# Differential attention in a two-layer decoder trunk: the order of mixing and rotation on VectorE, coefficients of three score tiles in one instruction, and rotary weight columns laid out by parity

## The chip, the cores and the metric

The kernel runs on one core of one Trainium2 chip. The metric is the device time of one execution in microseconds (us). A core has a matrix engine (TensorE, PE in the profile, with its weight loads as PEld), a vector engine (VectorE, DVE), an activation engine (ScalarE, ACT), a general engine (GpSimd, POOL) and a queue for transfers (SyncE, SP). Each works through its own list of instructions in the order in which it was written; engines wait for each other through semaphores.

## What is computed

The trunk has two layers over 512 tokens of width 1024. Each layer is a half-step SwiGLU feed-forward block, a token mixer, a cross-attention into 256 memory tokens and a second feed-forward block, each followed by a layer norm. The mixer of layer 0 is the differential attention; that of layer 1 is a pooling mixer. The change lies in the attention alone:

```python
q, k, v = jnp.split(x @ w_qkv, 3, axis=-1)          # 8 heads, two halves of 64 for q and k
q, k = rope(q, cos, sin), rope(k, cos, sin)          # pairs (c, c + 32) in each half of 64
s = einsum('bqhcd,bkhcd->bhcqk', q, k) * 64 ** -0.5  # causal, two score maps per head
p = softmax(s, axis=-1)
a = p[:, :, 0] - lam * p[:, :, 1]                    # the mix
o = einsum('bhqk,bkhe->bqhe', a, v)                  # then a norm per head, and @ w_o
```

All is float32. Products are made of two float32r parts: a high part (a rounded copy) and a low part (the rest), and three matmuls of parts take the place of one.

## The kernel before

The attention runs as two streams that one loop weaves into each other. The main stream (`da_main`) projects, for each pair of heads, the values `v` (two PSUM tiles of two token tiles each) and then per head the query `q` and the key `k`, each over 8 slices of the width in 24 matmuls. For the last pair of heads the values come after the keys. The side stream (`da_side`) does the attention of a head that was projected some time before: scores (`sc`) and their masks with the row maximum, exponentials, mix, transposes of the mixed tiles (`pt` from `p`), product with the values (`po`), scaling (`o`), and the turn of the head before (`pt` from `o`, then `oT`). A clock of estimated matmul time says after how many matmuls of the main stream the next step of the side stream is put in.

A head has four score tiles (query tiles 0 to 3), which are 128, 256, 384 and 512 columns wide, with two maps `p[0]` and `p[1]` each. For each map VectorE subtracts the mask and finds the maximum (`L1171`), and ScalarE takes the exponential and its row sum (`L1174`) into `sd`. `da_mix` then makes, per tile, a reciprocal `rc` of one sum (`L1187`), a coefficient `cf` (`L1188`), and `p[0] = p[1] * cf + p[0]` (`L1189`). It is told to stand behind the last mask of the head, and nothing else. TensorE then transposes the mixed tile (`L506`, `pt` from `p`), ScalarE and VectorE split the result into high and low part (`a`, `L135` and `L136`), and TensorE multiplies these by the values (`L1210`, `L1211`).

Rotation (`da_rope`) of a projected query or key: VectorE swaps the partners within groups of 32 partitions (`L1129`, a stream shuffle from PSUM), multiplies the projection by the cosines (`L1130`, the last reader of the PSUM tile), GpSimd multiplies the swapped copy by the signed sines (`L1131`), and VectorE adds the two (`L1132`, the rotary sum). ScalarE and VectorE then split the sum into parts (`L140` and `L141` for a query, `L135` and `L136` for a key).

For partners to lie 16 partitions apart, `cols_rope` reorders the columns of the weights while it splits them: ScalarE makes the high part of 128x1024 (`L290`), VectorE the low part in two halves of 128x512 (`L293`). Heads 0 to 5 use these lines; the same function serves heads 6 and 7.

The projections `q`, `k`, `v` and later the sums `ps` share one pool of two PSUM tiles. A third projection takes the tile whose readers are taken to be done first, and its first matmul waits for them.

What sets the order: a scheduler writes each engine's list before the program runs, from the order of the code, from dependencies and from costs that it assumes. `issue_after(x)` and `queue_behind(y, x)` say that an instruction may not stand ahead of `x` on its engine, with no wait. `high_priority()` puts instructions ahead of others that are free at the same point.

Of the kernel before, what the change touches and what calls it, by code (L numbers as in the profile page):

```python
# [9 lines left out]
F32 = mybir.dt.float32  # L10
# [3 lines left out]
ALU = mybir.AluOpType  # L14
# [3 lines left out]
P = 128  # L18
D = 1024
S = 512  # L20
NT = S // P
# [64 lines left out]
def shape_constants():  # L86

    p = np.arange(P)
    ident = np.eye(P, dtype=np.float32)
    mask = np.where(p[None, :] > p[:, None], np.float32(NEG), np.float32(0.0)).astype(np.float32)  # L90

    quarter, half, e = (p // 32) % 2, (p // 16) % 2, p % 16
    inv = np.array(INV_FREQ_BITS, dtype=np.uint32).view(np.float32)
    rope = np.stack([inv[quarter * 16 + e], np.where(half == 0, -1.0, 1.0)], axis=1).astype(np.float32)

    band = np.zeros((P, 4, 2, BAND), np.float32)
    t = np.arange(BAND)
# [12 lines left out]
def drain(units):  # L110
    for _ in units:
        pass
# [7 lines left out]
class Trunk:  # L120
# [80 lines left out]
    def mm(self, name):  # L201
        return self.mmp.tile([P, S], F32, tag="mm", name=name)
# [81 lines left out]
    def cols_rope(self, raw, j, wait=False):  # L284

        nc = self.nc
        w = self.hl([P, 8, P])
        src = raw[:, j].rearrange("p k (m h q e) -> p (k m) q h e", m=2, h=2, q=2)
        hi, lo = (t.rearrange("p k (m q h e) -> p (k m) q h e", m=2, q=2, h=2) for t in w)
        nc.scalar.copy(hi, src)  # L290
        with self.tc.issue_after(self.turned[1].ins) if wait else nullcontext():
            for q in range(2):
                self.last_low = nc.vector.tensor_sub(  # L293
                    lo[:, :, q], src[:, :, q], hi[:, :, q].bitcast(F32)
                )
        return w

    def wide(self, raw):
# [827 lines left out]
    def da_rope(self, ps):  # L1126
        nc = self.nc
        t1, t2 = self.tmp("rt"), self.tmp("rt")
        nc.vector.stream_shuffle(t2, ps, [(i + 16) % 32 for i in range(32)])  # L1129
        nc.vector.tensor_tensor(t1, ps, self.ropeC, ALU.mult)  # L1130
        nc.gpsimd.tensor_tensor(t2, t2, self.ropeS, ALU.mult)  # L1131
        nc.vector.tensor_tensor(t1, t1, t2, ALU.add)  # L1132
        return t1

    def da_query(self, ps):
# [11 lines left out]
    def da_scores(self, st, before):  # L1147

        nc = self.nc
        q, k, mm, terms = st["q"], st["k"], self.nc.tensor.matmul, ((0, 0), (1, 0), (0, 1))  # L1150
        one, two, three = ([self.aux("sc") for m in range(2)] for i in range(3))
        banks = {
            0: [t[:, 3 * P :] for t in two],
            1: [t[:, : 2 * P] for t in one],
            2: [t[:, : 3 * P] for t in two],
            3: three,
        }
        for i in SC_ORDER:
            qi, kn = slice(i * P, (i + 1) * P), slice(0, (i + 1) * P)
            for a, b in terms:  # L1160
                for m, rows in enumerate(HALVES):
                    mm(banks[i][m], q[a][rows, qi], k[b][rows, kn], start=a == b, stop=b == 1)
        for i in SC_ORDER:
            n = (i + 1) * P
            mx, rc, cf = self.small("mx"), self.small("rc", (P, 1)), self.small("cf", (P, 1))
            sm = st["sm"][:, i]
            p = [self.tmp("p")[:, :n] for m in range(2)]
            with self.tc.high_priority():
                for m in range(2):
                    least = mx[:, m : m + 1]  # L1170
                    st["masked"] = nc.vector.tensor_tensor_reduce(  # L1171
                        p[m], banks[i][m], self.mask[:, S - n :], -1.0, -NEG, ALU.add, ALU.min, least
                    )
                    exp = nc.scalar.activation(  # L1174
                        p[m], p[m], AF.Exp, bias=least, scale=-1.0, accum_out=sm[:, m : m + 1]
                    )
                if i == 2 and before:
                    with self.tc.issue_after(exp.ins):
                        self.da_scale(before)
            st["m", i] = p, sm, rc, cf  # L1180

    def da_mix(self, st, i):

        nc = self.nc
        p, sm, rc, cf = st.pop(("m", i))
        with self.tc.issue_after(st["masked"].ins):
            nc.vector.reciprocal(rc, sm[:, 1:2])  # L1187
            nc.vector.scalar_tensor_tensor(cf, sm[:, 0:1], self.nlam, rc, ALU.mult, ALU.mult)  # L1188
            nc.vector.scalar_tensor_tensor(p[0], p[1], cf, p[0], ALU.mult, ALU.add)  # L1189
        st["p", i] = p[0]  # L1190

    def da_turn(self, st, i):
# [55 lines left out]
    def da_main(self):  # L1248

        w, w_o = self.a["da_w_qkv"][0], self.a["da_w_o"][0]  # L1250
        self.turn_late(1)
        for n in range(0, DA_H, 2):
            vs = []
            if n < V_FIRST:
                yield from self.da_values(n, vs)
            rq, rk = self.raw_heads(w, n * P), self.raw_heads(w, D + n * P)
            for h in range(n, n + 2):
                q = self.mm("q")
                ws = self.cols_rope(rq, h % 2, h == 0)
                yield from self.project(q, ws)  # L1260
                q = self.da_query(q)
                k = self.mm("k")
                ws = self.cols_rope(rk, h % 2, h == 0)
                if h == 0:
                    with self.tc.issue_after(self.last_low.ins):
                        self.nlam = self.lam()
                yield from self.project(k, ws)
                k = self.da_key(k)
                sm = self.small("sd", (P, NT, 2))
                self.heads.append((self.clock, {"h": h, "q": q, "k": k, "v": vs, "sm": sm}))  # L1270
            if not vs:
                yield from self.da_values(n, vs)
        yield from self.to_tokens(self.oT[:4], w_o, 0, 4, True, False, ALPHA)
# [26 lines left out]
    def diff_attention(self, layer, ln):  # L1300
        self.mask = self.act("mask", (P, S), mybir.dt.bfloat16)
        self.nc.gpsimd.memset(self.mask[:, : S - P], 0.0)
        self.nc.gpsimd.tensor_copy(self.mask[:, S - P :], self.maskr)
        self.heads, self.oT = [], [None] * DA_H
        self.weave(self.da_main(), self.da_side(), GAP)
# [459 lines left out]
```

## Time and profile before

| | us |
|---|---|
| median of 3 runs | 1912.29 |
| lowest and highest | 1911.85 and 1914.07 |
| span of the profiled execution | 1913.0 |
| TensorE busy in it | 1894.9 (99%) |
| VectorE busy in it | 1550.6 (81%) |
| ScalarE busy in it | 1003.8 (52%) |
| granted TensorE clock, mean | 0.999 of full |

The attention takes about 345 to 560 us of the span. In the rows of the timeline the first number is the start in us from the span's start, the second the duration; then come engine, line, operation, output and inputs, shape and count, and in brackets how long the engine stood idle before it and what released it. An engine may begin its next instruction a little before the recorded end of the last one: on VectorE some 0.08 us, on ScalarE some 0.1 us, and TensorE's matmuls of 512 columns begin 0.23 us apart and are drawn 0.39 us long.

### The profile page before, as it was taken

Reading aid. Unit: us, or ns where it says so; the run is one execution under the profiler, and the core shown is the slowest. Engines: PE = TensorE matmul, PEld = TensorE weight load, DVE = VectorE, ACT = ScalarE, POOL = GpSimd, SP = SyncE. Lnnn points to the kernel's source line nnn. Section 1 sums busy time; section 2 is a strip of 40 time slices with the busy share of each in tenths; the row PEclk is TensorE's granted clock in tenths of the full one; section 3 lists DMA queues with packets and bytes.
Section 4 is the critical chain, followed back from the end, with each engine's and each line's share of the span. In section 5 each row is a group of like instructions: output and inputs, shape, how many; then the busy total and the mean of one; then the engine's idle time right before and its main releaser. Section 6 shows DMA issues by size and latency. Waiting matters only on the chain.

```text
span 1913.0 us, 32564 instructions
## 1 busy us (share of the span) xinstructions
PE 1894.9 (99%) x13136; PEld 1733.1 (91%) x13136; DVE 1550.6 (81%) x2250; ACT 1003.8 (52%) x1546; POOL 317.3 (17%) x274
## 2 busy tenths in 40 slices
PE   9999999999999999999999999999999999999998
PEld 8999998888878888999998999999899889999997
DVE  7888889888867558889888988898787568898886
ACT  6555554566645435645554655455455436555552
POOL 3112120111110001221220311212130012211210
PEclk9999999999999999999999999999999999999999
DMA  9978772323225327987785687878344438877861
GB/s 248 216 166 187 166 146 82 91 67 89 89 67 155 111 66 198 182 179 162 144 192 179 109 179 165 183 163 184 111 133 133 134 87 171 178 159 166 188 132 56
DMA packets 246743, 277.96 MB, mean 145 GB/s; under 512 B 8256, under 2 KB 212544, under 8 KB 246592
## 3 DMA queue, kind: packets, MB, share of 16 engines
q0 software_dynamic: 92928, 92.29, 31.5%
q1 hardware_dynamic: 153664, 183.59, 30.0%
q8 instruction: 103, 1.69, 0.4%
q14 instruction: 48, 0.39, 0.1%
HBM read 273.75 MB, written 2.10 MB: 144 GB/s over the span
## 4 chain that ended last, share of the span: by engine, by line
PE 85%; DVE 10%; ACT 2%; DMA 1%; issue 1%; POOL 1%; SPq 0%; DVEq 0%; ACTq 0%; POOLq 0%
PE x L221 7%; PE x L220 7%; PE x L222 7%; PE ps L220 4%; PE z L221 4%; PE z L220 4%; PE z L222 4%; PE ps L222 4%; PE ps L221 4%; PE px L222 2%; PE px L220 2%; PE px L221 2%; PE pt L506 2%; PE y L222 2%; PE x L757 2%; PE xq L222 2%
## 5 line engine op out<-in xcount | busy, mean ns | idle before, releaser
L725 POOL DMA_DIRECT2D ra<-in_ffn_w_in_dram x132 | 170.7, 1314 | 982.3 <-DVE wl L732 966.5
L730 ACT CAST wh<-ra 128x1024 fp32r<-128x1024 f32 x176 | 185.1, 1053 | 208.0 <-PE x L221 63.3
L732 DVE TENSOR_TENSOR wl<-ra,wh 128x1024 fp32r<-128x1024 f32 x176 | 214.4, 1223 | 66.5 <-ACT wh L730 66.1
L220 PE MATMUL x<-xe,wh 128*128 128x256 f32 x704 | 195.0, 277 | 0.0
L221 PE MATMUL x<-xe,wh 128*128 128x256 f32 x704 | 194.8, 277 | 0.0
L222 PE MATMUL x<-xe,wl 128*128 128x256 f32 x704 | 194.8, 277 | 0.0
L730 ACT CAST wh<-rc 128x1024 fp32r<-128x1024 f32 x132 | 139.0, 1053 | 102.4 <-PE x L221 41.6
L135 ACT CAST wh<-b 128x1024 fp32r<-128x1024 f32 x112 | 117.8, 1052 | 130.4 <-PE x L221 66.1
L732 DVE TENSOR_TENSOR wl<-rc,wh 128x1024 fp32r<-128x1024 f32 x132 | 160.3, 1222 | 25.5 <-ACT wh L730 25.5
L136 DVE TENSOR_TENSOR wl<-b,wh 128x1024 fp32r<-128x1024 f32 x112 | 136.9, 1222 | 41.0 <-ACT wh L135 41.0
L220 PE MATMUL x<-xh,wh 128*128 128x256 f32 x536 | 148.7, 277 | 0.0
L221 PE MATMUL x<-xl,wh 128*128 128x256 f32 x536 | 148.3, 277 | 0.0
L222 PE MATMUL x<-xh,wl 128*128 128x256 f32 x536 | 148.3, 277 | 0.0
L220 PEld LDWEIGHTS x<-xe,wh 128*128 128x128 f32 x704 | 132.4, 188 | 1.3
L221 PEld LDWEIGHTS x<-xe,wh 128*128 128x128 f32 x704 | 132.3, 188 | 1.3
L222 PEld LDWEIGHTS x<-xe,wl 128*128 128x128 f32 x704 | 132.2, 188 | 0.0
L136 DVE TENSOR_TENSOR wl<-raw,wh 128x1024 fp32r<-128x1024 f32 x64 | 82.4, 1296 | 41.1 <-ACT wh L135 40.5
L221 PEld LDWEIGHTS x<-xl,wh 128*128 128x128 f32 x536 | 100.8, 188 | 0.7
L220 PEld LDWEIGHTS x<-xh,wh 128*128 128x128 f32 x536 | 100.7, 188 | 0.7
L222 PEld LDWEIGHTS x<-xh,wl 128*128 128x128 f32 x536 | 100.6, 188 | 0.0
L135 ACT CAST wh<-raw 128x1024 fp32r<-128x1024 f32 x64 | 66.4, 1049 | 61.0 <-PE xq L221 19.1
L220 PE MATMUL z<-xe,wh 128*128 128x256 f32 x352 | 97.5, 277 | 0.0
(447 smaller groups left out, 6266.0 us busy)
## 6 DMA issues: line engine op xcount, KB each, us to landing
ra<-in_ffn_w_in_dram POOLq DMA_DIRECT2D x132, 512.0 KB, 7.0
rc<-in_ffn_w_in_dram SPq DMA_DIRECT2D x88, 512.0 KB, 5.8
b<-in_ffn_w_out_dram SPq DMA_DIRECT2D x76, 512.0 KB, 4.8
ra<-in_ffn_w_in_dram SPq DMA_DIRECT2D x44, 512.0 KB, 4.7
rc<-in_ffn_w_in_dram POOLq DMA_DIRECT2D x44, 512.0 KB, 7.8
raw<-in_xa_wkv_dram SPq DMA_DIRECT2D x16, 1024.0 KB, 5.4
raw<-in_da_w_qkv_dram SPq DMA_DIRECT2D x16, 512.0 KB, 5.2
raw<-in_xa_wq_dram SPq DMA_DIRECT2D x8, 1024.0 KB, 5.7
```

What stands on the lines that cost most here:

```text
L135: self.nc.scalar.copy(hi, src),
L136: self.nc.vector.tensor_sub(lo, src, hi.bitcast(F32)),
L220: self.first_mm = mm(out, w[0], x[0], start=start, stop=False, skip_group_check=again)
L221: mm(out, w[0], x[1], start=False, stop=False, skip_group_check=again)
L222: self.last_mm = mm(out, w[1], x[0], start=False, stop=stop, skip_group_check=again)
L506: self.turns = [self.nc.tensor.transpose(pt[:, j], b, self.ident) for j, b in enumerate(blocks)]
L725: nc.gpsimd.dma_start(t, source(*block), accum_op=ALU.add)
L730: hi = nc.scalar.copy(v[0], raw)
L732: lo = nc.vector.tensor_sub(v[1], raw, v[0].bitcast(F32))
L757: self.last_mm = nc.tensor.matmul(ps[:, j], v[i][:, k, j * P : (j + 1) * P], x[l][:, k], start=n == i == l == 0, stop=n == 7 and i == 1, s ...
```

## The change

Four things are changed, all in the attention:

- `da_mix` makes the reciprocals and coefficients of tiles 0 to 2 in one instruction of 128x3 each, and those of tile 3 in one of 128x1. All of the mix has high priority.
- The rotary sum of a query that was projected before the scores of the head ahead of it is put behind the mix of tile 2.
- The columns of the rotary weights are reordered by parity (even columns in the first 32 partitions, odd ones in the next 32), so that the low part is one instruction of 128x1024. Its source is read with a step of two elements, as is that of the high part.
- The table of frequencies follows the new order.

```diff
-    rope = np.stack([inv[quarter * 16 + e], np.where(half == 0, -1.0, 1.0)], axis=1).astype(np.float32)
+    rope = np.stack([inv[2 * e + quarter], np.where(half == 0, -1.0, 1.0)], axis=1).astype(np.float32)
...
-        src = raw[:, j].rearrange("p k (m h q e) -> p (k m) q h e", m=2, h=2, q=2)
-        hi, lo = (t.rearrange("p k (m q h e) -> p (k m) q h e", m=2, q=2, h=2) for t in w)
+        src = raw[:, j].rearrange("p k (m r q) -> p (k m) q r", m=2, q=2)
+        hi, lo = (t.rearrange("p k (m q r) -> p (k m) q r", m=2, q=2) for t in w)
         nc.scalar.copy(hi, src)
         with self.tc.issue_after(self.turned[1].ins) if wait else nullcontext():
-            for q in range(2):
-                self.last_low = nc.vector.tensor_sub(
-                    lo[:, :, q], src[:, :, q], hi[:, :, q].bitcast(F32)
-                )
+            self.last_low = nc.vector.tensor_sub(lo, src, hi.bitcast(F32))
         return w
...
-        nc.vector.tensor_tensor(t1, t1, t2, ALU.add)
+        self.rope_sum = nc.vector.tensor_tensor(t1, t1, t2, ALU.add)
...
-            st["m", i] = p, sm, rc, cf
+            st["m", i] = p
+        self.scored += 1
+        st["late_sums"], self.late_sums = self.late_sums, []
...
-        p, sm, rc, cf = st.pop(("m", i))
-        with self.tc.issue_after(st["masked"].ins):
-            nc.vector.reciprocal(rc, sm[:, 1:2])
-            nc.vector.scalar_tensor_tensor(cf, sm[:, 0:1], self.nlam, rc, ALU.mult, ALU.mult)
-            nc.vector.scalar_tensor_tensor(p[0], p[1], cf, p[0], ALU.mult, ALU.add)
+        p = st.pop(("m", i))
+        with self.tc.high_priority(), self.tc.issue_after(st["masked"].ins):
+            if i in (0, NT - 1):
+                n = slice(0, NT - 1) if i == 0 else slice(i, NT)
+                rc, st["cf"] = self.small("rc", (P, NT)), self.small("cf", (P, NT))
+                rc, cf, sm = rc[:, n], st["cf"][:, n], st["sm"][:, n]
+                nc.vector.reciprocal(rc, sm[:, :, 1])
+                nc.vector.scalar_tensor_tensor(cf, sm[:, :, 0], self.nlam, rc, ALU.mult, ALU.mult)
+            cf = st["cf"][:, i : i + 1]
+            mixed = nc.vector.scalar_tensor_tensor(p[0], p[1], cf, p[0], ALU.mult, ALU.add)
+        if i == NT - 2:
+            for add in st["late_sums"]:
+                self.queue_behind(add, mixed)
         st["p", i] = p[0]
...
                 q = self.da_query(q)
+                if self.scored < h:
+                    self.late_sums.append(self.rope_sum)
```

What the scheduler makes of it shows in the engines' lists. The lines of the changed kernel are numbered up to 9 apart from those before: the shuffle is `L1126`, the rotary sum `L1129`, the mix `L1189` to `L1192`.

VectorE around the masks of head 2, before: the rotation of the query of head 3 stands ahead of the first mask, and the first tile to be mixed is tile 0 (128 columns).

```order
L1130 TENSOR_TENSOR rt<-q,ropeC 128x512
L293 TENSOR_TENSOR wl<-raw,wh 128x16x32
L1132 TENSOR_TENSOR rt<-rt 128x512
L293 TENSOR_TENSOR wl<-raw,wh 128x16x32
L141 SCALAR_TENSOR_TENSOR qk<-rt,qk 128x512
L1171 ISA p,mx<-sc,mask 128x128
...
L1187 RECIPROCAL rc<-sd 128x1 x3
L1188 SCALAR_TENSOR_TENSOR cf<-sd,nlam,rc 128x1 x2
L1189 SCALAR_TENSOR_TENSOR p<-p,cf 128x128
L1189 SCALAR_TENSOR_TENSOR p<-p,cf 128x256
L1188 SCALAR_TENSOR_TENSOR cf<-sd,nlam,rc 128x1
L1187 RECIPROCAL rc<-sd 128x1
```

The same place in the change:

```order
L1127 TENSOR_TENSOR rt<-q,ropeC 128x512
L292 TENSOR_TENSOR wl<-raw,wh 128x1024
L1167 ISA p,mx<-sc,mask 128x128
...
L1189 RECIPROCAL rc<-sd 128x3
L1190 SCALAR_TENSOR_TENSOR cf<-sd,nlam,rc 128x3
L1192 SCALAR_TENSOR_TENSOR p<-p,cf 128x256
L1192 SCALAR_TENSOR_TENSOR p<-p,cf 128x384
L1189 RECIPROCAL rc<-sd 128x1
L1192 SCALAR_TENSOR_TENSOR p<-p,cf 128x128
L1190 SCALAR_TENSOR_TENSOR cf<-sd,nlam,rc 128x1
L1129 TENSOR_TENSOR rt<-rt 128x512
L1192 SCALAR_TENSOR_TENSOR p<-p,cf 128x512
```

The sum and the split of the query have moved behind the mix, and tile 0 is mixed last of the first three, behind the reciprocal of tile 3. That order of the tiles is the same in all eight heads; the late sum is there in heads 0, 2, 4, 5 and 6.

TensorE at head 6, where the main stream projects the values of heads 6 and 7 (two tiles, `v_5736` and then `v_5867` in the change). Before, the second projection follows the first at once, and the transposes of head 6 stand between its matmuls; here are its last matmul ahead of the first transpose, and that transpose:

```order
L222 MATMUL v_5939<-wh_5792,xl_3487 128x256
L506 MATMUL pt_5961<-ident_78,p_5875 128x128 [waits DVE_49]
L220 MATMUL v_5939<-wh_5796,xh_3486 128x256
L221 MATMUL v_5939<-wl_5797,xh_3486 128x256
L222 MATMUL v_5939<-wh_5796,xl_3488 128x256
```

In the change all 14 transposes stand in one block between the two projections, and the first matmul of the second waits:

```order
L222 MATMUL v_5736<-wh_5732,xl_3488 128x256
L503 MATMUL pt_5907<-ident_78,p_5816 128x128 [waits DVE_49]
L503 MATMUL pt_5907<-ident_78,p_5816 128x128
L503 MATMUL pt_5978<-ident_78,p_5823 128x128 [waits DVE_49]
...
L503 MATMUL pt_6005<-ident_78,p_5834 128x128 [waits DVE_49]
L503 MATMUL pt_6005<-ident_78,p_5834 128x128 x3
L220 MATMUL v_5867<-wh_5728,xh_3485 128x256 [waits DVE_49,PE_49]
L221 MATMUL v_5867<-wl_5729,xh_3485 128x256
```

The instruction that this matmul waits for is VectorE's part of the split of the first projection: the second now takes the PSUM tile of the first, and no longer that of a key. At head 5 the lists moved in the same way: transposes and value products of head 5 that stood between matmuls of a key's projection now stand in one block ahead of it, and that projection's first matmul waits for VectorE.

VectorE at head 6, before, behind the mix of tile 2, and then in the change, behind the mix of tile 0 (`v` is the split in question):

```order
L1189 SCALAR_TENSOR_TENSOR p<-p,cf 128x384
L1188 SCALAR_TENSOR_TENSOR cf<-sd,nlam,rc 128x1
L1189 SCALAR_TENSOR_TENSOR p<-p,cf 128x512
L136 TENSOR_TENSOR v<-v 128x4x128
L136 TENSOR_TENSOR a<-pt,a 128x128
```

```order
L1129 TENSOR_TENSOR rt<-rt 128x512
L1192 SCALAR_TENSOR_TENSOR p<-p,cf 128x512
L136 TENSOR_TENSOR a<-pt,a 128x128
L1126 STREAM_SHUFFLE rt<-k 128x512
L136 TENSOR_TENSOR a<-pt,a 128x256
L141 SCALAR_TENSOR_TENSOR qk<-rt,qk 128x512
L136 TENSOR_TENSOR v<-v 128x4x128
L1127 TENSOR_TENSOR rt<-k,ropeC 128x512
```

The split of the values has moved behind a rotary sum, two splits of transposes, a shuffle of a key and the split of a query.

More of the change, by code (lines that the diff above doesn't have):

```diff
@@ L1164, in da_scores @@
             n = (i + 1) * P
-            mx, rc, cf = self.small("mx"), self.small("rc", (P, 1)), self.small("cf", (P, 1))
-            sm = st["sm"][:, i]
+            mx, sm = self.small("mx"), st["sm"][:, i]
             p = [self.tmp("p")[:, :n] for m in range(2)]
@@ L1304, in diff_attention @@
         self.heads, self.oT = [], [None] * DA_H
+        self.scored, self.late_sums = 0, []
         self.weave(self.da_main(), self.da_side(), GAP)
```

## The prediction

> **What bounds the kernel now.** The page comes first, then TensorE's waits inside the attention (330 to 600 us), then the timeline of the engines at each of its eight heads.
>
> ```profile
> PE 1894.9 (99%) x13136; PEld 1733.1 (91%) x13136; DVE 1550.6 (81%) x2250; ACT 1003.8 (52%) x1546; POOL 317.3 (17%) x274
> ...
> PE pt L506 <- DVE p L1189: 3.8, 5, 1.3
> ```
>
> TensorE is busy for 99% of the span, so work taken from VectorE is worth nothing by itself. What can be won lies in TensorE's waits, and in the attention nearly all of them are the second row: five transposes of mixed tiles wait 3.8 us for VectorE's mix. They are at heads 0 (twice), 2, 4 and 5. Heads 1 and 3 have a row without a wait; I need the times at which TensorE wanted these tiles.
>
> ```profile
> 377.54 0.33 PE L506 MATMUL pt<-ident,p 128*128 128x128 f32 x1 [0.21 <-DVE p L1189]
> 381.75 0.33 PE L506 MATMUL pt<-ident,p 128*128 128x128 f32 x1 [0.61 <-DVE p L1189]
> 398.25 0.27 PE L506 MATMUL pt<-ident,p 128*128 128x128 f32 x1
> 424.28 0.33 PE L506 MATMUL pt<-ident,p 128*128 128x128 f32 x1 [0.87 <-DVE p L1189]
> 445.29 0.27 PE L506 MATMUL pt<-ident,p 128*128 128x128 f32 x1
> 471.39 0.33 PE L506 MATMUL pt<-ident,p 128*128 128x128 f32 x1 [0.89 <-DVE p L1189]
> 494.66 0.33 PE L506 MATMUL pt<-ident,p 128*128 128x128 f32 x1 [1.26 <-DVE p L1189]
> ```
>
> The idle time in brackets counts from the drawn end of the last matmul. Matmuls of 512 columns start 0.23 us apart and are drawn 0.39 long, so a wait costs 0.16 more than the bracket says: 0.37, 0.77, 1.03, 1.05 and 1.42, together 4.6 us. More than that, 0.24% of the time, the change cannot win from them. TensorE wanted the tiles at 377.17 (head 0), 398.25 (1), 423.25 (2), 445.29 (3), 470.34 (4) and 493.24 (5).
>
> **The first transpose of heads 0 to 4.** Today tile 0 is mixed right behind the masks. In the new list its mix stands behind the reciprocal of tile 3, and that one waits for the last exponential:
>
> ```profile
> 378.22 0.17 DVE L1187 RECIPROCAL rc<-sd 128x1 f32<-128x1 f32 x1 [0.21 <-ACT p L1174]
> 398.36 0.16 DVE L1187 RECIPROCAL rc<-sd 128x1 f32<-128x1 f32 x1 [0.21 <-ACT p L1174]
> 424.96 0.16 DVE L1187 RECIPROCAL rc<-sd 128x1 f32<-128x1 f32 x1 [0.21 <-ACT p L1174]
> 445.52 0.16 DVE L1187 RECIPROCAL rc<-sd 128x1 f32<-128x1 f32 x1 [0.22 <-ACT p L1174]
> 472.07 0.16 DVE L1187 RECIPROCAL rc<-sd 128x1 f32<-128x1 f32 x1 [0.21 <-ACT p L1174]
> ```
>
> These are heads 0 to 4; VectorE stood waiting each time. From such a reciprocal to the transpose of tile 0 I count 0.48: 0.08 to issue it, 0.34 for 128 columns of mix, 0.06 for the signal. Against that, at heads 0, 2 and 4 the masks themselves come earlier, since the rotary sum, half of the low part and the query's split leave the queue ahead of them. How much, head 2 shows, and head 0 a second limit:
>
> ```profile
> 416.79 1.43 DVE L293 TENSOR_TENSOR wl<-raw,wh 128x512 fp32r<-128x512 f32 x1
> 416.38 1.29 POOL L1131 TENSOR_TENSOR rt<-rt,ropeS 128x512 f32<-128x512 f32 x1 [1.21 <-DVE rt L1129]
> 420.13 0.28 DVE L1171 CUSTOM_DVE_ANT_0 p<-sc,mask 128x128 f32<-128x128 f32 x1
> ...
> 358.38 1.29 POOL L1131 TENSOR_TENSOR rt<-rt,ropeS 128x512 f32<-128x512 f32 x1 [13.83 <-DVE rt L1129]
> 358.78 1.98 DVE L136 TENSOR_TENSOR wl<-raw,wh 128x1024 fp32r<-128x1024 f32 x1
> 360.68 0.68 DVE L1132 TENSOR_TENSOR rt<-rt 128x512 f32<-128x512 f32 x1
> ...
> 370.74 2.18 PE L1162 MATMUL sc<-qk 64*128 64x128 f32 x24
> 373.38 0.28 DVE L1171 CUSTOM_DVE_ANT_0 p<-sc,mask 128x128 f32<-128x128 f32 x1
> ...
> 485.89 0.33 PE L1162 MATMUL sc<-qk 64*128 64x128 f32 x2
> 487.40 0.29 DVE L1171 CUSTOM_DVE_ANT_0 p<-sc,mask 128x128 f32<-128x128 f32 x1 [2.72 <-PE sc L1162]
> ```
>
> A low part that meets GpSimd's product stands nearly still until that ends: the full one at 358.78 freed VectorE at 360.68, 1.01 after GpSimd's end (359.67). At head 2 GpSimd ends at 417.67, so the new low part is out of the way at 418.68 and the masks start there instead of at 420.13: 1.45 earlier, and so does everything up to the reciprocal. Head 4 has the same rows. At head 0 the scores limit it: a mask can start 1.51 after the first score (487.40 less 485.89), at 372.25 instead of 373.38, 1.13 earlier. At heads 1 and 3 nothing leaves the queue. So the new loss is
>
> - head 0: 378.22 - 1.13 + 0.48 - 377.17 = 0.40
> - head 1: 398.36 + 0.48 - 398.25 = 0.59
> - head 2: 424.96 - 1.45 + 0.48 - 423.25 = 0.74
> - head 3: 445.52 + 0.48 - 445.29 = 0.71
> - head 4: 472.07 - 1.45 + 0.48 - 470.34 = 0.76
>
> that is 3.2, against 0.37 + 0.77 + 1.03 + 1.05 = 3.2 today. **Heads 0 to 4: nothing won**; heads 1 and 3, which wait for nothing today, pay for the rest.
>
> **The low and high parts.** One instruction for two saves VectorE some 0.06 us each; reads with a step of two elements appear nowhere in this trace. Below, such a read costs nothing; above, as the worst that one element of two unused could do, twice the time. I take nothing, since the old source already jumped every 16 elements without a price (0.68 for 512 columns, as the plain `L1132`). [...]
>
> **Head 5.** The masks are on time there, and the last exponential is over when ScalarE begins to scale `o`:
>
> ```profile
> 492.12 1.27 ACT L1239 ACTIVATE o<-o,f 128x128 f32<-128x128 f32 x4
> ...
> 525.17 0.60 PE L506 MATMUL pt<-ident,p 128*128 128x128 f32 x4
> 499.99 0.28 PE L1210 MATMUL po<-v,a 128*128 128x256 f32 x1
> 500.34 0.22 PE L1211 MATMUL po<-v,a 128*128 128x128 f32 x1
> ...
> L136 DVE TENSOR_TENSOR wl<-raw,wh 128x1024 fp32r<-128x1024 f32 x12 | 16.3, 1362 | 1.4 <-ACT wh L135 1.4
> L1132 DVE TENSOR_TENSOR rt<-rt 128x512 f32<-128x512 f32 x16 | 10.9, 682 | 2.4 <-POOL rt L1131 2.4
> L1217 DVE TENSOR_TENSOR o<-o,po 128x256 f32<-128x256 f32 x16 | 6.6, 415 | 10.1 <-ACT o L1216 10.0
> L1129 DVE STREAM_SHUFFLE rt<-k 128x512 f32<-128x512 f32 x8 | 6.0, 745 | 0.0
> L141 DVE SCALAR_TENSOR_TENSOR oT<-pt,subg,oT 128x512 fp32r<-128x512 f32 x8 | 5.9, 743 | 1.7 <-ACT oT L140 1.7
> L136 DVE TENSOR_TENSOR a<-pt,a 128x384 fp32r<-128x384 f32 x8 | 4.4, 551 | 1.8 <-ACT a L135 1.6
> ```
>
> The reciprocal of tile 3 can start 0.12 after that (514.60 against 514.48 at head 6, below), tile 0 is there at 492.72. TensorE wants it four matmuls sooner than today (493.24 - 0.93 = 492.31) and loses 0.41 instead of 1.42. But then comes the block: nine matmuls of `q` and six transposes later (2.8 us) stand 7 transposes (0.11 each) and 17 products (0.117 each) in a row, so the key's projection would be due at 492.8 + 2.8 + 2.8 = 498.4. It waits for VectorE to read the last key's PSUM tile, and ahead of that read VectorE must do, from 492.58: a coefficient 0.13, the sum 0.60, 512 columns of mix 0.67, `a` of 128 columns 0.20, the shuffle 0.66, a low part 1.14, `a` of 256 0.33, the query's split 0.61, `oT` 0.66, `a` of 384 0.47, `o` 0.33, `a` of 512 0.61, and the read itself 0.60 and 0.14 to its signal (means of the rows less 0.08; 1.14 for a low part that meets nothing). That is 499.7 at the soonest: a loss of 1.3. If one of them meets GpSimd's product (1.29), 2.6. Between these ends I take 2.0, as the shuffle starts that product in the middle of the list. [...] **Head 5: 0.41 + 2.0 - 1.42 = +1.0** (from +0.3 to +1.6).
>
> **Head 6.** Today the second projection of values starts at 513.59, right behind the first, which waits for nobody. In the new list it waits for VectorE's split of the first, with 14 transposes ahead of it.
>
> ```profile
> 513.47 0.28 PE L222 MATMUL v<-wh,xl 128*128 128x256 f32 x1
> 514.48 1.27 ACT L1239 ACTIVATE o<-o,f 128x128 f32<-128x128 f32 x4
> 515.65 0.56 ACT L135 CAST v<-v 128x512 fp32r<-128x512 f32 x1
> 514.60 0.16 DVE L1187 RECIPROCAL rc<-sd 128x1 f32<-128x1 f32 x1 [0.22 <-ACT p L1174]
> 515.45 0.75 DVE L1189 SCALAR_TENSOR_TENSOR p<-p,cf 128x512 f32<-128x512 f32 x1
> 516.24 0.69 DVE L136 TENSOR_TENSOR v<-v 128x512 fp32r<-128x512 f32 x1
> ```
>
> The transposes take 14 x 0.11, so it is due at 515.13. VectorE, from 514.60: reciprocal 0.08, mix of tile 0 0.27, coefficient 0.13, sum 0.60, mix of tile 3 0.67, `a` of 128 0.20, shuffle 0.66: 517.21. The shuffle releases GpSimd's product, 517.4 to 518.69. `a` of 256, whose source is PSUM, goes through; the query's split has both inputs in SBUF and stands still, as `L293` did at 416.79, which freed VectorE 0.47 after GpSimd's end (1.35 later, less its drawn tail): 519.16. Then the values' split, 0.69, and 0.06: 519.9. The loss is 4.8; without the meeting with GpSimd the split of the query ends at 518.1 and the loss is 3.8. I take 4.8, because that row shows the meeting. ScalarE's part (515.65 today) is not what comes last. What follows gives nothing back: TensorE stays full, and the transposes and products only change places. **Head 6: +4.8.**
>
> **The sum.** 0.0 + 1.0 + 4.8 = +5.8 us. The profiled execution spans 1913.0, 0.7 above the median of 1912.29; I add to the median: **1918.1 us**, 0.3% slower. Own range: +0.3 and +3.8 give 1916.4, +1.6 and +4.8 with 0.5 for small waits in the blocks give 1919.2.
>
> **Rivals.** *The blocks cost nothing.* If VectorE reaches the values' split by 514.4 it is done when the transposes are; for that the nine instructions between tile 3's reciprocal and the split (4.6 us with the wait for GpSimd) would have to stand elsewhere or the matmul to wait for less than I read from the list. Then only the first transposes count: 0.0 + 0.41 - 1.42 = -1.0, 1911.3, no change that can be told. *All five waits go and no new one comes* (the mix would be ready whenever TensorE wants it): -4.6, 1907.7, faster. Decided by whether tile 0's mix ends before TensorE wants it; the rows of tile 3's reciprocal speak against it at every head. *The read with a step costs double*: the low part stands directly ahead of the masks at heads 0, 2 and 4, 1.14 each, 3.4 more: 1921.5.
>
> **How the numbers follow.** Forecast 0.68, no cost of the blocks 0.15, all waits gone 0.07, costly reads 0.10. A measurement of this kernel tells 0.2% (3.8 us) from no change: under 1908.5 faster, above 1916.1 slower. From the cases: faster 0.08, the same 0.17 (no cost of the blocks, and the forecast's low tail), slower 0.75. The range 1914.0 to 1922.0 leaves out the two cases that end below it (0.22, less their upper tails) and takes in costly reads.
>
> **What would show it.** Right: a new wait of some 3 us or more of TensorE at the second projection of values around 520 us, released by VectorE's split of `v`; waits of 0.2 to 0.6 (idle) at the first transpose of every head 0 to 4; the key's projection behind head 5 starting some 2 us late; the new low part at 1.2 us alone. Wrong: no wait at that projection, or low parts above 1.5 us where GpSimd is idle.

## The result, and the profile after

The changed kernel takes **1921.58 us** in the median of five executions (1920.54 to 1924.08), the kernel before 1912.29 (1911.67 to 1914.20): a ratio of 1.0048, 95% interval 1.0037 to 1.0059. Timed once more beside the kernel before, it took 1921.47 against 1913.07, a ratio of 1.0046 (1.0032 to 1.0059). So it is 8.4 to 9.3 us slower. The forecast was 1918.1 with a range of 1914.0 to 1922.0. The profiled execution of the changed kernel took 1920.54; its span is 1918.8.

The page and TensorE's waits inside the attention (330 to 600 us) of the changed kernel; the columns of a wait are the engine and its operation, who it waited for, us in total, times, and the longest:

```profile
PE 1896.4 (99%) x13136; PEld 1733.1 (90%) x13136; DVE 1550.5 (81%) x2202; ACT 1003.6 (52%) x1546; POOL 320.3 (17%) x274
...
PE pt L503 <- DVE p L1192: 3.7, 8, 0.8
PE v L220 <- DVE v L136: 2.8, 1, 2.8
PE po L1217 <- DVE a L136: 1.3, 1, 1.3
```

VectorE has 48 instructions less and is as busy as before (1550.5 against 1550.6 us). TensorE's waits for the mix add up to what they were (3.7 against 3.8), in eight places instead of five, and two new rows stand below them. One by one, in the timeline of TensorE (the five first transposes of heads 0 to 4, then head 5 twice, then head 6 three times):

```profile
376.56 0.33 PE L503 MATMUL pt<-ident,p 128*128 128x128 f32 x1 [0.24 <-DVE p L1192]
397.03 0.33 PE L503 MATMUL pt<-ident,p 128*128 128x128 f32 x1 [0.42 <-DVE p L1192]
422.82 0.33 PE L503 MATMUL pt<-ident,p 128*128 128x128 f32 x1 [0.57 <-DVE p L1192]
444.53 0.33 PE L503 MATMUL pt<-ident,p 128*128 128x128 f32 x1 [0.54 <-DVE p L1192]
470.33 0.33 PE L503 MATMUL pt<-ident,p 128*128 128x128 f32 x1 [0.54 <-DVE p L1192]
491.62 0.33 PE L503 MATMUL pt<-ident,p 128*128 128x128 f32 x1 [0.25 <-DVE p L1192]
497.81 0.33 PE L1217 MATMUL po<-v,a 128*128 128x128 f32 x1 [1.29 <-DVE a L136]
514.25 0.44 PE L503 MATMUL pt<-ident,p 128*128 128x128 f32 x2 [0.76 <-DVE p L1192]
516.52 0.33 PE L503 MATMUL pt<-ident,p 128*128 128x128 f32 x1 [0.34 <-DVE p L1192]
519.96 0.36 PE L220 MATMUL v<-wh,xh 128*128 128x256 f32 x1 [2.78 <-DVE v L136]
```

Where the time goes shows best in matmuls that both kernels issue at the same point of their work. Three of them, before: the first of the values of heads 0 and 1, the first of the query of head 6 (heads 0 to 4 are transposed by then), and one of the sums behind head 6:

```profile
339.22 0.36 PE L220 MATMUL v<-wh,xh 128*128 128x256 f32 x1
488.81 0.39 PE L220 MATMUL q<-xh,wh 128*128 128x512 f32 x1
527.64 0.45 PE L220 MATMUL ps<-wh,oT 128*128 128x512 f32 x1
```

and the same three in the change:

```profile
338.20 0.36 PE L220 MATMUL v<-wh,xh 128*128 128x256 f32 x1
487.72 0.39 PE L220 MATMUL q<-xh,wh 128*128 128x512 f32 x1
532.56 0.44 PE L220 MATMUL ps<-wh,oT 128*128 128x512 f32 x1
```

The change enters the attention 1.02 us sooner, stands 1.09 sooner after head 4 and 4.92 later after head 6. So heads 0 to 4 are worth 0.1 us, and heads 5 and 6 cost 6.0 together. Behind that the distance stays: 4.95 at the memory keys, where the attention is long over. The lead at the start is not the change's doing: at this point the profiled executions of all kernels run here lie up to 4.3 us apart, two of the kernel before 1.4.

VectorE (and GpSimd in the second row) at head 6 of the changed kernel, the shuffle of a key, GpSimd's product, the query's split and the values' split:

```profile
516.59 0.73 DVE L1126 STREAM_SHUFFLE rt<-k 128x512 f32<-128x512 f32 x1
517.40 1.26 POOL L1128 TENSOR_TENSOR rt<-rt,ropeS 128x512 f32<-128x512 f32 x1 [2.62 <-DVE rt L1126]
517.58 1.63 DVE L141 SCALAR_TENSOR_TENSOR qk<-rt,qk 128x512 fp32r<-128x512 f32 x1
519.13 0.68 DVE L136 TENSOR_TENSOR v<-v 128x512 fp32r<-128x512 f32 x1
```

The query's split starts 0.18 after the product, takes 1.63 where it takes 0.69 alone, and frees VectorE 0.47 after GpSimd's end (519.13 against 518.66). The values' split starts at 519.13 and TensorE at 519.96.

At head 5 of the changed kernel the meeting goes the other way round (low part, product, query's split, and the split of the 384-column `a` that TensorE waits for at 497.81):

```profile
493.72 1.21 DVE L136 TENSOR_TENSOR wl<-raw,wh 128x1024 fp32r<-128x1024 f32 x1
493.91 2.17 POOL L1128 TENSOR_TENSOR rt<-rt,ropeS 128x512 f32<-128x512 f32 x1 [2.63 <-DVE rt L1126]
495.18 1.45 DVE L141 SCALAR_TENSOR_TENSOR qk<-rt,qk 128x512 fp32r<-128x512 f32 x1
497.21 0.54 DVE L136 TENSOR_TENSOR a<-pt,a 128x384 fp32r<-128x384 f32 x1
```

The low part is first and takes its 1.21; the product takes 2.17 instead of 1.26, and the query's split, which starts while it still runs, 0.76 more than alone.

### The profile page after: what moved, and what is told of

Its sections match the earlier page's. It is cut to its first block, busy times and chain, and to the rows that moved or that the text cites. A ratio compares the mean times of both kernels' runs of the same rounds, so it can differ in the third digit from the quotient of the medians.

```text
span 1918.8 us, 32507 instructions
## 1 busy us (share of the span) xinstructions
PE 1896.4 (99%) x13136; PEld 1733.1 (90%) x13136; DVE 1550.5 (81%) x2202; ACT 1003.6 (52%) x1546; POOL 320.3 (17%) x274
## 4 chain that ended last, share of the span: by engine, by line
PE 84%; DVE 10%; ACT 3%; DMA 2%; issue 1%; POOL 0%; SPq 0%; DVEq 0%; ACTq 0%; POOLq 0%
PE x L220 7%; PE x L221 7%; PE x L222 7%; PE z L220 4%; PE z L222 4%; PE z L221 4%; PE ps L220 4%; PE ps L222 4%; PE ps L221 4%; PE px L220 2%; PE px L222 2%; PE px L221 2%; PE y L222 2%; PE y L221 2%; PE y L220 2%; PE xq L220 2%
## 5 line engine op out<-in xcount | busy, mean ns | idle before, releaser
L136 DVE TENSOR_TENSOR wl<-b,wh 128x1024 fp32r<-128x1024 f32 x112 | 136.6, 1220 | 41.0 <-ACT wh L135 41.0
L136 DVE TENSOR_TENSOR wl<-raw,wh 128x1024 fp32r<-128x1024 f32 x64 | 81.6, 1284 | 44.4 <-ACT wh L135 43.8
```

Of the source, the lines that this page charges most:

```text
L136: self.nc.vector.tensor_sub(lo, src, hi.bitcast(F32)),
```

## The experiments

All times below are medians beside runs of the kernel before on the same chip, whose medians were 1913.07 (the first four kernels below), 1913.30 (the parity layout alone, the values' split early, the mix without priority, a coefficient per tile) and 1912.84 (the other three).

**The two kernels once more.** The kernel before and the change, unaltered.

> The kernel before, unchanged, beside itself. The change measured 9.3 us slower, while the two profiles differ by 5.8 us, 5.9 of it inside the attention. Theory A (the waits of TensorE at heads 0 to 6 are all that the change costs, about 5.8 us; the rest is that the one profiled execution of before was a slow one): the spans of these runs have a median near 1910.5 us, 2.5 below the 1913.0 of the first profile, and a new profile that is shorter than 1913.0 is shorter outside the attention, ahead of 60 us. Theory B (3.5 us of the 9.3 belong to the change but do not show in its profile): the spans here lie near 1913.0 and the time near 1912.3.

> The change as it is, on the same chip as the runs beside it, so that the edits below can be compared with it. Theory A: 5 to 7 us slower than before when both are taken on one chip. Theory B: 9 us slower again. In its profile the same waits as in the first one: about 3.1 us at the first transposes of heads 0 to 4, 1.45 behind the block of head 5, 4.4 at head 6.

1913.36 (ratio 1.0001, 0.9992 to 1.0010) and 1921.47. The difference of the spans is now 8.2 us (1911.2 and 1919.4), where the first pair had 5.8. So neither theory holds as it stood. The new profile of the kernel before is 1.8 us shorter than the first, 1.4 of it ahead of the attention, as A has it; but the change is 8.4 us slower, more than A allows, and most of that does show in this profile. In it the waits are the same ones to 0.02 us, and the attention costs 7.5 us instead of 5.9. The windows of TensorE behind head 6 show what came on top; columns: stretch, its length, busy time (and instructions) of PE, PEld, DVE, ACT and POOL, the granted clock, and two of DMA. The second profile of the change, then the first:

```profile
518.03:521.44 3.41, 1.30 (x11) 1.33 (x12) 3.25 (x4) 0.02 (x1) 0.81 (x1) 1.00 0.03 5
521.44:524.85 3.41, 3.41 (x18) 3.41 (x18) 1.90 (x3) 1.64 (x3) 0.00 (x0) 0.50 0.00 0
```

```profile
518.20:521.61 3.41, 1.66 (x14) 1.69 (x15) 2.90 (x4) 0.37 (x1) 0.46 (x1) 1.00 0.02 5
521.61:525.02 3.41, 3.41 (x31) 3.41 (x31) 1.90 (x3) 1.84 (x4) 0.00 (x0) 1.00 0.00 0
```

For 3.41 us after the long wait TensorE is granted half its clock and begins 18 matmuls instead of 31; 13 matmuls of 256 columns, 0.117 each, are 1.5 us. By that a stretch of 3.41 at half clock loses at most 1.7, half of its length. The mean clock was 0.999 in two of the ten executions of the change (1920.09 and 1920.54) and 0.996 to 0.998 in eight, whose median is 1921.5. In all 72 executions of the kernel before beside these experiments it was 0.999. Half of 3.41 us is 0.0009 of 1919 us, and the trace with one such stretch has 0.998; so the 0.997 and 0.996 of seven executions point to two or three stretches. That is an estimate, since no trace of such an execution was kept.

**Without the late sums of heads 5 and 6.** The rotary sum goes behind the mix at heads 0, 2 and 4 only.

```diff
-                if self.scored < h:
+                if self.scored < h < 6:
```

> The change, but the rotary sum is put behind the mix only for the queries of heads 1, 3 and 5 (mixes of heads 0, 2 and 4), not for those of heads 6 and 7. My theory: the blocks at heads 5 and 6 come from those two late sums, so they dissolve: TensorE's waits of 1.45 us behind the block of head 5 and of 4.4 us at head 6 go, head 5 loses 1.2 to 1.4 at its first transpose as before the change, heads 0 to 4 keep their 3.1. Result: 4.5 to 5.5 us faster than the change, within 1 us of the kernel before. Rival (the blocks come from the priority of the mix or from the low part in one piece): the wait at the second projection of values stays at 2.8 us and the time is that of the change.

1913.09 (ratio 1.0002, 0.9994 to 1.0011): no longer slower. The waits of heads 5 and 6 shrink to one transpose (0.91 idle at head 5), the others stay:

```profile
PE pt L503 <- DVE p L1192: 3.2, 6, 0.9
```

So with the mix as it stands in the change, the late sums at heads 5 and 6 are what makes it slower, by 8.4 us, more than I expected: some 5 are the waits (0.41 + 1.45 + 4.4 in the change, 0.16 added to each bracket, against 1.07 here), and the clock comes on top: it is 0.999 in ten of eleven executions here. What the late sums cost with another order of the mix, the last two kernels below show.

**The same, with tile 0 mixed first.**

```diff
+            if i:
+                self.queue_behind(mixed, st["mixed"])
+            st["mixed"] = mixed
```

> The run above, and the mixes of a head are told to stand in the order of the tiles, so that tile 0 is mixed first, ahead of the reciprocal of tile 3. My theory: the first transposes of heads 0 to 4 lose 3.1 us because tile 0's mix waits for the last exponential; with tile 0 first they wait for next to nothing, since at heads 0, 2 and 4 the masks come 1.1 to 1.45 us sooner than before, and at heads 1 and 3 the kernel before had no wait. Result: 2.5 to 3.5 us faster than the run above and 2 to 3.5 us faster than the kernel before (about 1909). Rival (TensorE's first transposes are held by something else, for instance by ScalarE or the masks): the waits stay near 0.5 each and the time stays that of the run above.

**1910.14** (ratio 0.9984, 0.9976 to 0.9993): faster than both kernels, by 2.9 us.

```profile
PE pt L503 <- DVE p L1192: 0.8, 1, 0.8
```

No first transpose of heads 0 to 4 waits any more; one at head 5 is left. Against the run above only the order of the mixes differs in the code, TensorE's list has one transpose in another place, and it is worth 3.0 us: the loss of 3.2 that the prediction put down to tile 0 standing behind the reciprocal of tile 3.

**The parity layout alone.** The kernel before with the reordered columns and their table of frequencies, and nothing else of the change (cut, `...`).

```diff
-        src = raw[:, j].rearrange("p k (m h q e) -> p (k m) q h e", m=2, h=2, q=2)
...
+        src = raw[:, j].rearrange("p k (m r q) -> p (k m) q r", m=2, q=2)
...
-            for q in range(2):
-                self.last_low = nc.vector.tensor_sub(
-                    lo[:, :, q], src[:, :, q], hi[:, :, q].bitcast(F32)
-                )
+            self.last_low = nc.vector.tensor_sub(lo, src, hi.bitcast(F32))
```

> The kernel before with the parity layout alone: one low part of 128x1024 whose source is read with a step of two, in place of two halves of 128x512. My reading: the step costs nothing (in the changed kernel these low parts took 1.21 at the least, those with a contiguous source 1.21 as well), so what is left is that a whole low part stands still when it meets GpSimd's product, and then stands ahead of the masks of heads 0, 2 and 4: up to 0.5 more at each of their first transposes, 0 to 1.6 in all, 1913.1 to 1914.7 us. Rival: the step makes these 16 low parts and ScalarE's 16 high parts cost the path more than that (1.14 more each at three heads): 1916.5 us.

1915.83 (ratio 1.0014, 1.0005 to 1.0023), slower by 2.5 us (1.0 to 4.4), a little above the upper end of my reading; the rival's price lies inside the interval. The trace decides between them. First the reads themselves, the low parts in the changed kernel from 345 us on (shortest, median and longest in ns; `L292` reads with a step of two, `L136` does not), and ScalarE's high parts before and after:

```profile
L292 DVE TENSOR_TENSOR wl<-raw,wh x16: 1210/1272/2037, 346.8 to 463.2; 128x1024 fp32r<-128x1024 f32 x16
L136 DVE TENSOR_TENSOR wl<-raw,wh x10: 1206/1224/1968, 357.8 to 525.6; 128x1024 fp32r<-128x1024 f32 x10
```

```profile
L290 ACT CAST wh<-raw x16: 1032/1049/1057, 336.9 to 462.4; 128x1024 fp32r<-128x1024 f32 x16
...
L290 ACT CAST wh<-raw x16: 1092/1128/1166, 335.9 to 461.7; 128x1024 fp32r<-128x1024 f32 x16
```

On VectorE the step is free in these rows (1.21 and 1.21 us at the least), and on ScalarE the new order costs 0.08 us of 1.05 (medians). The loss lies in the order. VectorE ahead of the masks of head 2, in the second profile of the kernel before and in this one:

```profile
415.38 1.43 DVE L293 TENSOR_TENSOR wl<-raw,wh 128x512 fp32r<-128x512 f32 x1
416.74 0.68 DVE L1132 TENSOR_TENSOR rt<-rt 128x512 f32<-128x512 f32 x1
417.34 0.68 DVE L293 TENSOR_TENSOR wl<-raw,wh 128x512 fp32r<-128x512 f32 x1
418.12 0.69 DVE L141 SCALAR_TENSOR_TENSOR qk<-rt,qk 128x512 fp32r<-128x512 f32 x1
418.73 0.28 DVE L1171 CUSTOM_DVE_ANT_0 p<-sc,mask 128x128 f32<-128x128 f32 x1
```

```profile
414.08 1.97 DVE L292 TENSOR_TENSOR wl<-raw,wh 128x1024 fp32r<-128x1024 f32 x1
415.97 0.68 DVE L1129 TENSOR_TENSOR rt<-rt 128x512 f32<-128x512 f32 x1
417.35 0.69 DVE L141 SCALAR_TENSOR_TENSOR qk<-rt,qk 128x512 fp32r<-128x512 f32 x1 [0.70 <-ACT qk L140]
417.96 0.28 DVE L1168 CUSTOM_DVE_ANT_0 p<-sc,mask 128x128 f32<-128x128 f32 x1
```

From low part to mask it is 3.35 before and 3.88 here. The second half used to fill the time in which ScalarE makes the query's high part; now VectorE stands idle there for 0.70, while the whole low part holds the sum back longer. The first transposes of heads 0, 2 and 4 wait 0.5 more each, 1.6 us in the trace; of the other 0.9 no row tells. In the change itself this price is not paid, since sum and split have left that place.

**The values' split early.** High priority for the split that the long wait at head 6 ends with.

```diff
-            self.split(v[:, :, :, 0], v[:, :, :, 1], ps)
+            with self.tc.high_priority():
+                self.split(v[:, :, :, 0], v[:, :, :, 1], ps)
```

> The change, with high priority also for VectorE's split of the values; at head 6 the split then stands ahead of the mix and no longer behind the query's split. My reading: the single wait of 2.8 idle at the second projection of values goes (to at most 0.4); the transposes ahead of it wait 0.4 to 0.8 more than they did, so 2.5 to 3.4 are won there, and 0.7 is lost at heads 1 and 3, where the split now stands ahead of the mix as well. And the half-speed stretch of TensorE's clock, which I put down to the long wait, is gone: mean clock 0.999 in every execution, 1.5 more won. Time 1916 to 1918 us. Rival: the lower clock belongs to the change, not to this wait: still 0.997 in most executions, and 1918 to 1919.5 us.

1918.09 (ratio 1.0021, 1.0012 to 1.0029): 3.4 us less than the change. The wait for `v` is gone, and the first transposes of heads 1 and 3 wait 0.47 and 0.46 more than in the change (0.89 and 1.00 idle):

```profile
PE pt L503 <- DVE p L1193: 4.3, 7, 1.0
PE po L1218 <- DVE a L136: 1.3, 1, 1.3
```

The time lies just above my reading and in the range of the rival; the wait went as I expected, the clock did not. It was 0.999 in four of eleven executions (median 1916.7) and 0.998 in seven (1918.3), so something besides the wait of 2.8 lowers it.

**The same kernel again, for a trace with the lower clock.**

> The kernel with the values' split early, once more, for its trace: seven of its eleven executions had a mean clock of 0.998. If the clock falls because of the idle time in one stretch of some 3.4 us, a trace with 0.998 shows the half-speed stretch right behind head 5's block or among head 6's transposes, where the idle time of 3.4 us reaches 1.2 or more; if the clock falls for another reason, the stretch lies elsewhere. A trace with 0.999 shows none.

One execution, 1918.28, with 0.998. The half-speed stretch is there, 499.38 to 502.80. It stands right behind head 5's block, whose wait of 1.29 ends at 497.96, and not at head 6, where I had put its cause:

```profile
495.97:499.38 3.41, 2.12 (x16) 1.60 (x13) 3.41 (x7) 1.84 (x7) 0.26 (x1) 1.00 0.00 0
499.38:502.80 3.42, 3.42 (x11) 2.67 (x10) 3.34 (x7) 0.62 (x1) 0.71 (x1) 0.50 0.33 59
```

**The late sum left out at head 5 alone, and at head 6 alone.**

The first diff leaves it out at head 5, the second at head 6 (`h` is the head whose query is projected).

```diff
-                if self.scored < h:
+                if self.scored < h != 6:
```

```diff
-                if self.scored < h:
+                if self.scored < h < 7:
```

> The change, with the late sum left out at head 5 alone (the sum of the query of head 6 goes back ahead of the masks); heads 0, 2, 4 and 6 keep theirs. TensorE's list then has the block of head 6 and not that of head 5. My reading: the two blocks are separate. Against the kernel with late sums at heads 0, 2 and 4 only (1913.1 us) the second projection of values waits again, 4.2 to 4.5 with the waits ahead of it, and the clock falls after it in most executions, 1 to 1.5 more: 1918 to 1919 us, mean clock 0.997 or 0.998 in most. Rival: the two blocks hang together (the long wait at head 6 comes from the delay that head 5 leaves on VectorE): then the wait at head 6 is under 1 and the time 1913 to 1914.5 us.

> The change, with the late sum left out at head 6 alone; heads 0, 2, 4 and 5 keep theirs. TensorE's list has the block of head 5 and not that of head 6. My reading: no wait at the second projection of values; head 5's block costs some 1 to 1.5 against 1913.1 us, and the first transpose of head 6 waits 0.5 to 1.7 for a mix that comes later: 1914.5 to 1916 us, with the clock at 0.999 in every execution if only the long wait of head 6 lowers it. Rival for the clock: the block of head 5, with 1.3 idle among short matmuls, lowers it too: 0.998 in a good part of the executions.

Without head 5's: 1919.44 (ratio 1.0033, 1.0021 to 1.0046), 0.4 us above my reading, mean clock 0.997 or 0.998 in all six executions. The wait at the second projection of values is 2.8 (idle), as long as in the change, so it does not come from head 5, and the rival falls.

Without head 6's: 1917.79 (ratio 1.0026, 1.0016 to 1.0037), 2 to 3 us more than I expected, clock 0.998 in two of seven. The wait for `v` is not there, head 5's is, and the first transpose of head 6 waits 1.01 (idle), where it waits for nothing without both late sums:

```profile
PE po L1217 <- DVE a L136: 1.3, 1, 1.3
```

```profile
496.27:499.68 3.41, 2.12 (x13) 1.64 (x14) 3.41 (x7) 1.39 (x6) 0.00 (x0) 1.00 0.00 0
499.68:503.09 3.41, 3.41 (x10) 2.63 (x9) 3.33 (x6) 0.62 (x1) 1.15 (x1) 0.50 0.39 97
```

Each block costs by itself and each can lower the clock. Against 1913.1 they cost 4.7 (head 5) and 6.3 (head 6) alone and 8.4 together; the intervals of the ratios are 2 to 2.6 us each way, so whether they add up is not shown. Of the 4.7, the attention of its profile shows 4.1, at most 1.7 of it half speed and 1.2 the wait at head 6; the executions at full clock are nearly as slow (median 1917.4), and some 2 us of them I have not found.

**The mix without high priority, and a coefficient per tile.** Two ways to undo half of what put tile 0 last: the first takes `high_priority()` from the mix, the second makes `rc` and `cf` per tile as before and keeps the priority. In both lists tile 0 is mixed first.

```diff
-        with self.tc.high_priority(), self.tc.issue_after(st["masked"].ins):
+        with self.tc.issue_after(st["masked"].ins):
```

```diff
-            if i in (0, NT - 1):
-                n = slice(0, NT - 1) if i == 0 else slice(i, NT)
...
+            rc, st["cf"] = self.small("rc", (P, 1)), self.small("cf", (P, 1))
+            cf, sm = st["cf"], st["sm"][:, i]
```

> The change without the high priority of the mix. In VectorE's list tile 0 is then mixed first of its three again, ahead of the reciprocal of tile 3; the late sums and the blocks of heads 5 and 6 stay. My reading: the first transposes of heads 0 to 4 wait for nothing (3.1 won), heads 5 and 6 keep some 2 and 3.5 to 5: 1916.5 to 1918.5 us, with the clock at 0.997 where the wait at head 6 is near 3 idle. Rival: the first transposes wait for the masks and not for tile 0's place in the list; then they still wait 0.3 to 0.6 each and the time is 1919 to 1920 us.

> The change with a reciprocal and a coefficient per tile, as before; priority, late sums and parity stay. In VectorE's list tile 0 is mixed first here too, and the values' split at head 6 stands two instructions sooner. My reading: no wait at the first transposes of heads 0 to 4 (3.1 won), the blocks of heads 5 and 6 cost 5 together instead of 6 to 7, with no wait of over 1.5 at once, so the clock stays up (1.5 won): 1914 to 1916 us. Rival: if three coefficients at once save VectorE time that counts, it is worse than that: 1918 us or more.

1916.18 (ratio 1.0013, 1.0004 to 1.0022) and 1913.13 (0.9996, 0.9987 to 1.0006), both a little better than expected. No first transpose of heads 0 to 4 waits in either, so it was the place in the list and not the masks. What is left are the blocks and, without priority, a wait of 0.80 (idle) at a later transpose of head 0. Without priority the blocks show as

```profile
PE v L220 <- DVE v L136: 1.6, 1, 1.6
PE k L220 <- DVE rt L1127: 1.3, 1, 1.3
```

and with a coefficient per tile as

```profile
PE v L220 <- DVE v L136: 1.0, 1, 1.0
PE v L220 <- DVE rt L1127: 0.9, 1, 0.9
```

The first has the lower clock in nine of ten executions, the second in none. With a coefficient per tile, the trace reaches the first of the values of heads 0 and 1 at 336.81, the query of head 6 at 483.05 and the same sum behind head 6 at 524.99: against the kernel before, heads 0 to 4 win 3.3 us and heads 5 and 6 lose 3.1. So the same late sums of heads 5 and 6 cost some 3 us with a coefficient per tile and some 6 without priority (1913.13 and 1916.18 against the 1910.14 of the kernel that has tile 0 first and not these two sums), where they cost 8.4 in the change: their price depends on how the mix around them is ordered. Three coefficients in one instruction, with priority, let VectorE take the longer tiles 1 and 2 ahead of tile 0; either half alone does not.

## Why the prediction was right, and what it left out

**What bounds the kernel**: right. VectorE lost 48 instructions and TensorE got nothing from it. The most that could be won was put at 4.6 us; the best version here wins 2.9 (its attention 4.1 in the traces).

**Heads 0 to 4, nothing won**: right, head by head. With 0.16 added to the brackets the first transposes wait 0.40, 0.58, 0.73, 0.70 and 0.70 us, where 0.40, 0.59, 0.74, 0.71 and 0.76 were forecast; the matmuls put the sum of the five heads at -0.1. That tile 0's place is the cause, the run with tile 0 first shows (3.0 us).

**The low and high parts, nothing**: right for the sum and for VectorE's read (1.21 with the step as without); the rival of a costly read falls, although its 1921.5 is the time that came out. ScalarE's high parts, made from the same source, take 8% longer (1.128 against 1.049 us in the median). That one instruction for two halves can delay the masks by 0.5 I had not costed as a loss; in this change the sum and split that it delayed have left that place.

**Head 5, +1.0**: the size was right, the waiting instruction was not. Up to the first matmul of the values that follow (504.35 before, 505.03 after) the change falls back by 1.8, with five value products more already done (0.6), so 1.2. The wait was to be at the key's projection, for the read of its PSUM tile; it stands at a value product, for the 384-column `a` (1.29). The projection itself starts at 499.33, and the forecast's 498.4 less the lead of 1.09 is 497.3: 2.0 late, as forecast. Only 1.45 of this is the wait. The other 0.6 is the block itself, which was counted at 5.6 us and takes 6.3 without its wait (491.62 to 499.33, less 1.45); a wait that was put too long and a block that was put too short made up for each other. The forecast's VectorE list was right up to there. The upper end of its range counted 1.29 for a meeting with GpSimd's product; in the trace such a meeting holds VectorE up by 0.76: the low part, first by 0.19, takes its 1.21, the product 2.17 instead of 1.26, and the query's split 1.45 instead of 0.69. At head 6 the product is first, by 0.18, and takes its 1.26, and the split takes 1.63.

**Head 6, +4.8**: right. 6.0 for both heads less 1.2 is 4.8. VectorE was to reach the values' split at 519.16 and did at 519.13. That these agree so closely is in part luck: the forecast started from today's 514.60 without the loss at head 5, and the change came to head 6 with a lead of 1.09 that made up for it (its reciprocal of tile 3 starts at 514.65). The meeting with GpSimd, which the forecast took from the row at 416.79, is what the trace shows (0.47 in both). The `a` of 256 columns, whose source is PSUM, takes 0.42 from 517.24 with the product running from 517.40; in the kernel before it takes 0.42 from 498.00, and `oT`, from PSUM too, 0.75 from 498.32 (0.74 in the mean of eight), inside a product that runs from 498.25 to 499.54.

**The sum**: +5.8 forecast, +5.9 in the attention of the first two profiles. The difference came out 2.6 to 3.5 us larger (8.4 and 9.3), and one term was missing: the sum counted waits and took TensorE's clock as full. The clock is halved for 3.41 us at least once in eight of ten executions of the change, if their mean clocks (0.996 to 0.998) are read by the one trace with 0.998: behind the wait of 2.8 in the trace above, and behind head 5's block in the traces of two kernels that keep that block. By the medians of executions with and without, the lower clock costs 1.2 us in the change (eight and two), 1.6 with the values' split early (seven and four) and 2.3 without head 6's late sum (two and five). The rest, 1 to 2 us, is not settled: the two executions of the change at full clock are 7.0 and 8.3 slower than the medians before beside them (1920.09 against 1913.07, 1920.54 against 1912.29), not 6; but single executions of the kernel before lie between 1911.1 and 1916.7, so two cannot decide it.

**The range**: partly luck. The range of the sum itself ended at 1919.2, below the 1921.5 that was measured. The time lies within 1914.0 to 1922.0 because the range was widened for the costly read, which the runs refute, and not for the clock.

## What to carry to other kernels

An instruction that is moved behind others on its engine takes everything queued behind it along: the late sum freed the masks of three heads and held up, at two others, a split that TensorE was waiting for (1.29 and 2.78 us idle); so a late placement belongs only where nobody waits for what follows. How much it costs hangs on the rest of the list: with the mix arranged in two other ways, the same late sums cost some 3 and some 6 us instead of 8.4. Priority acts on instructions that are free at the same point, so making them free together (one coefficient instruction for three tiles) changes their order too; where one of them is needed first, say so. And price a new wait on TensorE with its clock: behind waits of 1.3 to 2.8 us, the executions with the lower clock took 1.2 to 2.3 us more than those without.

## What the runs showed of the hardware that I had not expected

The half-speed stretches in four traces are 3.41 or 3.42 us long: 521.44 to 524.85 (the second trace of the change), 499.68 to 503.09 (without head 6's late sum), 499.38 to 502.80 (the values' split early) and 514.80 to 518.22 (the mix without priority). In the 3.41 us directly ahead of them TensorE was idle for 2.1, 1.3, 1.3 and 1.8. Of two profiles of the change with the same waits, 1.3 at head 5 and 2.8 at head 6 (idle), one has such a stretch and one has not: the first has full clock from 490 to 560 us, the second through the wait at head 5 and up to 521.44. So waits of this length are followed by half clock in some traces and not in others; what beside them decides these runs leave open, and so does this: the mean clock was also 0.998 in two of eleven executions of the parity layout alone and in one of eleven without the late sums of heads 5 and 6, whose traces show no single wait over 1.42 and 0.91 (idle).
